# Rank scatter on one core: 14 of 128 tiles as row copies and all loads in halves of 10 KB

## The chip, the core and the metric

The kernel runs on one core of one Trainium2 chip. The metric is device time in microseconds (us) of one execution. "The span" is the time from the first to the last instruction in the profile, about 2 us less. Executions of the kernel before agree within 0.2%.

## The reference

```python
B, N, D = 8, 2048, 2560                      # x: B x N x D float32, scores: B x N
order = np.argsort(scores, axis=1)
ranks = np.argsort(order, axis=1)            # rank of each row within its batch
out[np.arange(B)[:, None], ranks, :] = x     # row i of a batch goes to row rank(i)
```

16,384 rows of 10 KB are read and written once, each to a place that the scores decide. Ranks are counted on VectorE by comparing every score of a batch with all others; that part is done by about 435 us and is not on the path at the end. What matters here is how rows are moved.

## The kernel before

There are two ways for a row. The *bulk* works in groups of 256 rows (2 tiles of 128): GpSimd issues a load into SBUF, 20 KB a partition, and two indirect DMAs that scatter the rows by rank. The *row copies* go from DRAM to DRAM, one DMA a row, issued by SyncE and ScalarE, with the target's address in a register.

```python
GROUPS = [(256 * i, 2) for i in range(8)]        # (first row, rows a partition)
DIRECT = range(6)                                # batches whose group 0 is row copies
BULK = [(b, g) for b in range(B) for g in range(len(GROUPS)) if g or b not in DIRECT]
NBUF, LAG, G = 8, 4, 16
THIN = [(b, 4) for b in range(1, B)]             # groups whose scatter skips 4 partitions
HOLES = range(48, 48 + 4)                        # those partitions: 8 single row copies a group
HALVED = range(8)                                # bulk groups loaded in two DMAs of 10 KB a partition
# ... load of bulk group k:
for j in range(m if k in HALVED else 1):
    part = slice(j * D, (j + 1) * D) if k in HALVED else slice(0, m * D)
    line.eng.dma_start(out=xb[k % NBUF][:, part], in_=rows[:, part]).then_inc(sem, 16)
# ... row copies; the two sequencers, sp (SyncE) and act (ScalarE), take half a group each:
todo = list(enumerate(THIN))
for b in DIRECT:
    while todo and todo[0][1][0] < b:
        n, where = todo.pop(0)
        thin_rows(n, *where)                     # single row copies, sp and act in turns
    for h, (line, name) in enumerate(((sp, ENG.SP), (act, ENG.Activation))):
        line.after(dve, t_rows[b])
        half = WIDE // 2                         # 128
        with line.eng.Fori(0, half // G) as q:   # a loop on the sequencer
            _, at = nc.values_load_multi_w_load_instructions(   # 16 addresses to registers
                rows_i[b][:, bass.ds(half * h + q * G, G)], engines=[name], ...)
            for i in range(G):
                row = b * N + GROUPS[0][0] + half * h + i
                line.eng.dma_start(
                    out=out_bytes[bass.ds(at[i], ROW)],
                    in_=x_bytes[bass.ds(q * (G * ROW) + row * ROW, ROW)],
                ).then_inc(s_rows[line], 16)
for n, where in todo:
    thin_rows(n, *where)
```

## Time and profile before

| | kernel before |
|---|---|
| time, median (range) | 782.2 us (782.1 to 783.2) |
| span of the profiled run | 779.7 us |
| row copies: SyncE, ScalarE | 800, 792 |
| bulk groups | 58 |
| last row copy issued / last bulk packet / last row packet | 765 / 769.4 / 775.4 us |

The prediction below shows the page's DMA rows, one stretch of the DMA view and the order of time of the two issuing queues. In the DMA view, q0 is the bulk, q1 and q10 are the row copies of SyncE and ScalarE; its columns are packets, MB, and the time of those packets as a share of 16 engines. In the order of time a line is: start, length, engine, source line, operation, tensors, count. "SPq" and "ACTq" are the sequencers of SyncE and ScalarE. L402 is the DMA of the looped row copies, L376 that of the single ones, L391 the load of 16 addresses into registers.

### The profile page before, as it was taken

The numbers are of one execution on the slowest core, as the hardware profiler recorded it, in microseconds if no ns is written. First come the engines' busy times: TensorE is split into PE (matmuls) and PEld (weight loads), VectorE is DVE, ScalarE is ACT, GpSimd is POOL, SyncE is SP. The second block draws the span as 40 slices with busy tenths as digits, with TensorE's granted clock in tenths as the row PEclk, the third lists the DMA queues.
The fourth block names the chain that finished last, engine by engine and source line by source line (L and its number), as shares of the span: only waits on it lengthen the run. The fifth ranks groups of instructions, "written<-read, shape, count | busy, mean of one in ns | idle before, by whom it ended". The sixth has DMA issues, their size and how long they took to land.

```text
span 779.7 us, 8177 instructions
## 1 busy us (share of the span) xinstructions
PE 35.4 (5%) x170; PEld 30.5 (4%) x170; DVE 399.8 (51%) x825; ACT 0.0 (0%) x1; POOL 150.2 (19%) x189
## 2 busy tenths in 40 slices
PE   4000020020020020120000000000000000000000
PEld 4000010010010010120000000000000000000000
DVE  5999979979979979899999200000000000000000
ACT  0000000000000000000000000000000000000000
POOL 4113122212121211112121212121212121220100
PEclk9999995555555555565555555555555555555555
DMA  8999999999999999999999999999999999999995
GB/s 360 418 419 419 426 415 425 415 421 416 424 418 424 416 421 417 425 417 423 419 421 420 422 419 421 420 422 422 417 425 416 426 416 425 417 424 418 419 415 101
DMA packets 77186, 320.15 MB, mean 411 GB/s; under 512 B 28448, under 2 KB 53920, under 8 KB 53920
## 3 DMA queue, kind: packets, MB, share of 16 engines
q0 software_dynamic: 25920, 300.90, 90.7%
q1 hardware_dynamic: 25904, 10.93, 5.5%
q10 hardware_dynamic: 25344, 8.16, 4.5%
q14 instruction: 17, 0.14, 0.0%
q8 instruction: 1, 0.02, 0.0%
HBM read 168.41 MB, written 168.35 MB: 432 GB/s over the span
## 4 chain that ended last, share of the span: by engine, by line
DMA 49%; another core or an unknown queue 19%; DVE 13%; POOL 7%; issue 6%; PE 1%; POOLq 0%; SPq 0%
DMA out_dram<-x,rank_i 43%; DVE trash L238 12%; DMA x<-in_x_dram 6%; POOL out_dram L422 5%; POOL x L126 1%; PE ps_all L196 0%; DVE s_all L339 0%; DMA s_in<-in_scores_dram 0%; PE ps_col L175 0%; POOLq L446 0%; DVE rank_i L276 0%; DVE rank L270 0%; DVE rank L264 0%; PE ps_row L298 0%
## 5 line engine op out<-in xcount | busy, mean ns | idle before, releaser
L238 DVE TENSOR_SCALAR_CACHE_REDUCE trash<-s_all,s_col 128x1792 bf16<-128x1792 f32 (+7 forms) x240 | 315.2, 1348 | 4.6
L422 POOL DMA_INDIRECT out_dram<-x,rank_i x116 | 112.7, 972 | 141.8 <-DMA x<-in_x_dram 36.4
L126 POOL DMA_DIRECT2D x<-in_x_dram x64 | 35.7, 560 | 445.7 <-DMA out_dram<-x,rank_i 426.6
L238 DVE SCALAR_TENSOR_TENSOR trash<-s_all,s_col,mask 128x256 bf16<-128x256 f32 x128 | 61.6, 481 | 0.0
L196 PE MATMUL ps_all<-ident,s_col 128*128 128x128 f32 x128 | 28.5, 416 | 3.1 <-DVE s_all L339 2.8
L196 PEld LDWEIGHTS ps_all<-ident,s_col 128*128 128x128 f32 x128 | 26.8, 226 | 4.2 <-DVE s_all L339 3.2
L298 PE MATMUL ps_row<-ident,rank 128*1 128x128 f32 x26 | 7.0, 366 | 392.5 <-DVE rank_i L284 335.2
L339 DVE COPY s_all<-ps_all 128x512 f32<-128x512 f32 x32 | 20.2, 685 | 1.7 <-PE ps_all L196 1.4
L238 DVE DVE_READ_ACCUMULATOR trash<-s_all,s_col 128x1 f32 x240 | 19.9, 83 | 0.0
L298 PEld LDWEIGHTS ps_row<-ident,rank 128*1 128x1 f32 x26 | 1.9, 95 | 395.8 <-DVE rank_i L284 337.6
L238 DVE DVE_READ_ACCUMULATOR trash<-s_all,s_col,mask 128x1 f32 x128 | 10.6, 83 | 0.0
L309 DVE TENSOR_SCALAR thin_i<-ps_row 1x8 int32<-1x8 f32 x7 | 1.1, 154 | 17.7 <-PE ps_row L298 17.7
L324 DVE TENSOR_SCALAR rows_i<-ps_row 1x256 int32<-1x256 f32 x6 | 2.5, 412 | 4.1 <-PE ps_row L298 4.1
L183 DVE COPY s_col<-ps_col 128x128 f32<-128x128 f32 x1 | 0.3, 290 | 4.5 <-PE ps_col L175 4.5
L175 PE MATMUL ps_col<-ident,s_in 8*128 8x8 f32 x16 | 2.1, 262 | 3.6 <-DMA s_in<-in_scores_dram 3.6
L175 PEld LDWEIGHTS ps_col<-ident,s_in 8*128 8x128 f32 x16 | 2.0, 211 | 3.6 <-DMA s_in<-in_scores_dram 3.6
L276 DVE CAST rank_i<-rank 128x16 int32<-128x16 f32 (+3 forms) x11 | 1.9, 173 | 0.4
L270 DVE TENSOR_TENSOR rank<-rank,acc 128x16 f32<-128x16 f32 (+3 forms) x11 | 1.9, 170 | 0.4
L264 DVE TENSOR_TENSOR rank<-acc,acc 128x16 f32<-128x16 f32 (+3 forms) x11 | 1.9, 170 | 0.4
L284 DVE TENSOR_SCALAR rank_i<-rank,hole 128x2 int32<-128x2 f32 x7 | 1.6, 228 | 0.2
L156 POOL TENSOR_SCALAR_AFFINE_SELECT mask<-mask 128x256 f32<-128x256 f32 x2 | 0.8, 398 | 0.0
L168 DVE MEMSET acc<- 128x128 f32 x1 | 0.2, 165 | 1.1 <-SPq L102 1.1
(10 smaller groups left out, 1.8 us busy)
## 6 DMA issues: line engine op xcount, KB each, us to landing
x<-in_x_dram POOLq DMA_DIRECT2D x50, 2560.0 KB
x<-in_x_dram POOLq DMA_DIRECT2D x14, 1280.0 KB
out_dram<-in_x_dram SPq DMA_DIRECT2D x800, 10.0 KB
out_dram<-in_x_dram ACTq DMA_DIRECT2D x792, 10.0 KB
x<-in_x_dram SPq DMA_DIRECT2D x2, 1280.0 KB, 9.3
out_dram<-x,rank_i POOLq DMA_INDIRECT x116, 48.4
s_in<-in_scores_dram SPq DMA_DIRECT2D x1, 64.0 KB
```

Of the source, the lines that this page charges most:

```text
L126: line.eng.dma_start(out=xb[k % NBUF][:, part], in_=rows[:, part]).then_inc(sem, 16)
L175: nc.tensor.transpose(out=ps_col[:, B * c:B * (c + 1)], in_=s_in[:, r + j:r + m * P:m], identity=ident[:B, :B],)
L196: nc.tensor.transpose(out=ps_all[:, P * c:P * (c + 1)], in_=s_col[:, c, b:b + 1].to_broadcast([P, P]), identity=ident[:],)
L238: do(out=trash[i][:, :P * (hi_c - lo_c)], in0=s_all[:, P * lo_c:P * hi_c], accum_out=acc[i][:, col:col + 1], **how,)
L264: nc.vector.tensor_tensor(out=rank[:, cols], in0=acc[0][:, cols], in1=acc[1][:, cols], op=OP.add)
L270: nc.vector.tensor_tensor(out=rank[:, cols], in0=rank[:, cols], in1=acc[2][:, cols], op=OP.add)
L276: nc.vector.tensor_copy(out=rank_i[:, cols], in_=rank[:, cols])
L284: nc.vector.tensor_scalar(out=rank_i[:, cols], in0=rank[:, cols], scalar1=hole[:], scalar2=None, op0=OP.add,)
L298: nc.tensor.transpose(out=ps_row[:1, P * j:P * (j + 1)], in_=rank[:, col:col + 1], identity=ident[:],)
L324: nc.vector.tensor_scalar(out=rows_i[b][:].rearrange("o (p j) -> o p j", p=P), in0=ps_row[:1, :WIDE].rearrange("o (j p) -> o p j", p=P), s ...
L339: nc.vector.tensor_copy(out=s_all[:, 512 * q:512 * (q + 1)], in_=ps_all[:, 512 * q:512 * (q + 1)],)
L422: nc.gpsimd.indirect_dma_start(out=out_flat, out_offset=bass.IndirectOffsetOnAxis(ap=rank_i[:, col:col + 1], axis=0), in_=xb[k % NBUF][:, ...
```

## The change

One more group of 256 rows and 8 more single rows go to the row copies, and all loads are cut in two. The intent is to take rows off the bulk's way through SBUF, and to give the row copies more turns on the DMA engines by making the bulk's packets smaller.

```diff
-    DIRECT = range(6)
+    DIRECT = range(7)
-    THIN = [(b, 4) for b in range(1, B)]
+    THIN = [(b, 4) for b in range(1, B)] + [(3, 6)]
-    HALVED = range(8)
+    HALVED = range(len(BULK))
-            while todo and todo[0][1][0] < b:
+            while todo and (todo[0][1][0] < b or b == DIRECT[-1]):
```

The last line moves the single row copies that are left ahead of the last loop.

## The prediction

> **What bounds the kernel now.** I read the page first, its DMA rows above all, then the DMA view cut to stretches, then the order of time of the two queues that issue the row copies, then single packets and single issues in the trace.
>
> ```profile
> DMA  8999999999999999999999999999999999999995
> GB/s 360 418 419 419 426 415 425 415 421 416 424 418 424 416 421 417 425 417 423 419 421 420 422 419 421 420 422 422 417 425 416 426 416 425 417 424 418 419 415 101
> ...
> q0 software_dynamic: 25920, 300.90, 90.7%
> q1 hardware_dynamic: 25904, 10.93, 5.5%
> q10 hardware_dynamic: 25344, 8.16, 4.5%
> ```
>
> The 16 DMA engines are full from the first slice to the last but one. q0 carries the bulk, issued by GpSimd: load a group of 256 rows into SBUF, scatter it by rank. q1 (SyncE) and q10 (ScalarE) carry the row copies, DRAM to DRAM, 800 and 792 of them. Those two are the short queues in bytes but not in packets, and the DMA view of 440 to 640 us shows why:
>
> ```profile
> DMA packets 19793, 84.05 MB, mean 420 GB/s; under 512 B 7349, under 2 KB 13945, under 8 KB 13945
> ...
> q0 software_dynamic: 6596, 79.77, 93.6%
> q1 hardware_dynamic: 6597, 2.12, 4.2%
> q10 hardware_dynamic: 6597, 2.12, 4.2%
> ```
>
> The three queues get the same number of packets: each engine serves them in turn, one packet each. A row is 16 pieces of 640 B, one an engine, and a semaphore write of 4 B behind each: two packets an engine. A group is 8 load packets of 20 KB, 16 scatter packets of 10 KB and 3 semaphore packets an engine, 27 in all, so a queue gets 13.5 rows through in each group's 13.2 us: 0.98 us a row. That is the service limit of a row queue.
>
> The other limit is issue, and the order of time of the two queues shows it:
>
> ```profile
> 19.44 233.36 SPq L402 DMA_DIRECT2D out_dram<-in_x_dram  x256
> ...
> 507.67 244.95 SPq L402 DMA_DIRECT2D out_dram<-in_x_dram  x256
> 753.57 11.37 SPq L376 DMA_DIRECT2D out_dram<-in_x_dram  x16
> 19.40 342.35 ACTq L402 DMA_DIRECT2D out_dram<-in_x_dram  x384
> ```
>
> A sequencer's first loops run at 233.36/256 = 0.91 and 342.35/384 = 0.89 us a row, its later ones at 0.96. Rows issued less rows served, counted by me from issues and 640 B packets, is 2 to 6 up to 120 us, grows from there, and stays at 32 to 34 in each queue from about 360 us. So up to 360 us a queue runs at the pace at which its sequencer can issue; only then is its ring full and the turn-taking sets the pace. One block of ScalarE, read off in order, shows the issue cost: 16 DMA instructions of 0.53 us, each with one ALU operation and two moves (0.09 us) and 0.12 us between them, 0.74 us a row; then 1.9 us for the branch and the load of 16 row addresses into registers. That is 13.7 us for 16 rows, 0.86 us a row, with nothing to wait for. The source view agrees:
>
> ```profile
> L402 ACTq DMA_DIRECT2D out_dram<-in_x_dram x768: 418/530/1403, 19.4 to 749.6; - x192
> L391 ACTq TENSOR_LOAD <-rows_i x48: 1007/1488/2682, 18.0 to 735.8; - x48
> ```
>
> The ends nearly coincide: SyncE issues its last row at 765 us, q0's last packet is at 769.4, q1's at 775.4, the span ends at 779.7. The kernel is balanced: bulk and row copies run out together.
>
> **What the Trainium skill says.** Page "DMA: Bandwidth & Descriptors". Section "Queues, rings and completion order": an engine goes round the queue rows it has work for, packet by packet; the trace agrees (6596, 6597, 6597), and here a packet is one piece of 640 B to 20 KB. Section "Issuing engines are not separate DMA queues": issuing from several engines saves only sequencer time, "which is usually small relative to the DMA itself". For these row copies the trace says the opposite: 0.86 us to issue a row whose 32 packets take 16 x (32 + 9) = 656 ns of engine time, 0.04 us on 16 engines. Section "Latency and other measured facts": a register load [...]has a floor of about 0.6 us; here it is 1.0 us for 16 addresses and up to 2.7.
>
> **The change part by part.**
>
> *More row copies.* Batch 6's first group moves from bulk to row copies: 128 rows more for each queue. One more group leaves out four partitions (8 rows, to ScalarE). Rows a queue: 7 x 128 + 32 = 928 on both, against 800 and 792. On the engines this is nearly free. Removed from q0: 256 row loads and 264 row scatters; added: 264 rows. A 10 KB scatter packet takes 385 ns, a 20 KB load 761, so a bulk row costs about 766 ns of engine time against 656 to 709 for a row copy (709 is the mean with its slow packets at the end). About -12 engine-us, under 1 us of time.
>
> *All loads halved.* 49 or 50 more groups load in packets of 10 KB. Two of 385 ns replace one of 761, 9 to 11 ns more (means 386.5 and 762.1); times 6400 packets is 58 to 70 engine-us, plus one semaphore packet an engine and group, 7. Over 16 engines +4 to +5 us. What it buys is turns: a group now has 16 + 16 + 4 = 36 packets an engine, so the service limit of a row queue goes from 0.98 to 0.775 us a row (a group would take 36 turns, 13.95 us, for 18 rows). This is plainly the intent: without it 928 rows could not be served in 780 us.
>
> *The bulk's end.* 28,864 packets of 386.5 ns and 3,680 of 9 ns on q0 and 110 us of q1's first loads make 11,300 engine-us, 706 us on 16 engines. Overlapping packets sum to 1.022 of the time in the middle; two row queues at 0.9 us a row take 0.098 of it; 706/0.924 = 764, plus the start at 6.7: the bulk ends at about 770 us, where it does now.
>
> *The rows' end.* The service limit falls below the issue cost, so the row queues become issue-bound for the whole run, and nothing in the change makes issuing cheaper. From 160 to 360 us, steady and with rings not yet full, the DMA view counts:
>
> ```profile
> out_dram<-in_x_dram SPq DMA_DIRECT2D x231, 10.0 KB
> out_dram<-in_x_dram ACTq DMA_DIRECT2D x227, 10.0 KB
> ```
>
> 200/229 = 0.87 us a row. Before 160 us it is slower, where GpSimd issues groups at twice the usual pace (7 us apart; blocks of 15 to 17 us against 13.5 to 14): 146 rows of SyncE by 160 us. The rest is 928 - 146 = 782 rows, times 0.87 = 680: last issue at 840. Corrections, estimated: the blocks' register loads (1.0 to 2.6 us) and DMA instructions lengthen with GpSimd's issues, which become four a group and not three, +0.01 us a row or +7; after 770 GpSimd and the bulk are gone and blocks should take 13.5, -3. Last issue at about 844. The last row then needs about 4 us to its packets (the first rows did: issued 19.4, first packet 23.3 to 23.7), and the kernel 4.4 us from its last packet to the end, as now (775.4 to 779.7): span about 852. Runs last 2 us longer than the span (781.5 for 779.7): about **854 us**, and 9% slower.
>
> *Single rows ahead of the last loop.* All eight address sets are ready by about 435 us, when VectorE ends; the queues get there at about 710, so nobody waits. It moves 32 rows a queue from the end to before the last loop and saves nothing while the issue stream is the path. VectorE gains two small operations (0.23 and 0.15 us), TensorE two transposes, off the path.
>
> **The rivals.**
> 1. *The bulk is the bound* and the rows fit beside it. Then only halving and tail count: +4 - 1, less up to 4 us of today's tail (770 to 775.4, where a few engines work off row copies at a DMA share of 0.27, 0.13, 0.06): 779 to 786 us. For it: engines 100% busy now, and service at 0.775 would finish 928 rows by 745. Against: rows would have to be issued at 0.82 us each from 19.4 to 780, and blocks with empty rings took 13.5 to 17 us for 16; none was under 13.1.
> 2. *Issue at its floor.* The slow blocks could be due to the ring after all, and vanish once service is faster. With 13.3 us a block: 56 x 13.3 = 745, four sets of single rows at 6.8 = 27, start 18: 790, plus 8 and 2: 800 us. For it: the fastest blocks, 13.2 to 13.5. Against: slow blocks at 60 to 130 us with a backlog of 2 to 8 rows, so no full ring.
> 3. *Issue gets worse.* The double pace of GpSimd's issues before 130 us made blocks of about 15.5. If four issues a group act like that throughout, 56 x 15.3 + 27 + 18 = 902 to the last issue before the bulk-free end takes some 8 off: 905 us. Against: four issues in 13.5 us are still well below six in 14.
>
> **Range and chances.** The centre is the measured steady issue rate; 0.84 us a row (the fastest steady stretch of 40 us has 48 rows, 0.83) gives 782 x 0.84 + 160 + 10 = 827, 0.90 gives 874. Range 826 to 880. Faster by 2% needs under 766.5, below even the bulk's end: 0.02. Within 2%, up to 798, needs every block at its floor: 0.06. Slower: 0.92.
>
> **What would show it.** Right: the page's DMA digits fall to 1 or 2 in the last four slices with GB/s in the tens; q0's last packet stands at 765 to 775 us; GpSimd's last scatter issue at 730 to 745; SyncE's and ScalarE's loops show 0.85 to 0.92 us a row and end after 820; q1 and q10 have fewer packets than q0 in a middle stretch, not equal ones; the rows issued and not served stay under 10. Wrong: equal packets on all three queues in the middle, or loops under 0.82 us a row (then rival 1 or 2), or q0's last packet well past 785 (the bulk itself got slower).

## The result

| | before | after |
|---|---|---|
| time, median (range) | 782.2 us (782.1 to 783.2) | 838.8 us (831.1 to 847.8) |
| ratio of fast runs, 95% interval | | 1.069 (1.060 to 1.078) |
| span of the profiled run | 779.7 us | 840.6 us |
| rows issued by SyncE, ScalarE | 800, 792 | 928, 928 |
| last bulk packet | 769.4 us | 763.4 us |
| last row packet | 775.4 us | 839.0 us |

The change costs 7%. Ratios here are the mean time of one kernel's fast runs over that of the other's fast runs of the same rounds, so not quite the ratio of the medians quoted. One run of four, at 847.8 us, counts as slow for being over 1.5% above the fastest; its granted clock, 0.522, is that of fast ones, so it may be no more than the far end of this spread.

The page after, its DMA rows (tenths of busy time in 40 slices of 21 us, GB/s, then the queues):

```profile
DMA  8999999999999999999999999999999999992111
GB/s 363 418 417 421 417 418 419 417 418 417 418 418 417 418 418 417 418 418 418 418 417 417 418 418 418 418 418 418 419 417 418 419 418 418 417 417 56 26 24 17
...
q0 software_dynamic: 32544, 295.58, 83.1%
q1 hardware_dynamic: 30000, 12.25, 5.6%
q10 hardware_dynamic: 29696, 9.56, 4.8%
```

For 36 slices the engines are as full as before; in the last three they move 17 to 26 GB/s. The view of stretches puts numbers on it (stretch, length, busy time by engine, clock, DMA share, GB/s):

```profile
740.00:750.00 10.00, 0.00 (x0) 0.00 (x0) 0.00 (x0) 0.00 (x0) 0.00 (x0) 0.50 1.03 417
765.00:780.00 15.00, 0.00 (x0) 0.00 (x0) 0.00 (x0) 0.00 (x0) 0.00 (x0) 0.50 0.17 25
800.00:820.00 20.00, 0.00 (x0) 0.00 (x0) 0.00 (x0) 0.00 (x0) 0.00 (x0) 0.50 0.15 24
```

From 765 us the engines are at least 83% idle and no compute engine works. What still works is the issuing, as the order of time of the two queues shows:

```profile
19.56 232.86 SPq L402 DMA_DIRECT2D out_dram<-in_x_dram  x256
...
492.41 223.75 SPq L402 DMA_DIRECT2D out_dram<-in_x_dram  x256
...
732.19 105.77 SPq L402 DMA_DIRECT2D out_dram<-in_x_dram  x128
...
719.77 106.60 ACTq L402 DMA_DIRECT2D out_dram<-in_x_dram  x128
```

The first loops run as before (232.9 us for 256 rows, before 233.4), the third at 0.87 us a row where the kernel before had 0.96, and the last one at 0.83, most of it with nearly empty DMA engines. SyncE issues its last row at 838.0 us and the span ends at 840.6. That the turns no longer bind shows in the DMA view of 440 to 640 us:

```profile
q0 software_dynamic: 8690, 78.88, 93.2%
q10 hardware_dynamic: 7470, 2.41, 4.8%
q1 hardware_dynamic: 7247, 2.33, 4.7%
```

Before, the three counts were equal. Now the row queues leave 14% and 17% of the turns unused. Rows issued less rows served, counted as in the prediction, stay under 7 throughout; before, from 360 us on, they were 28 to 35, in the median 32 or 33.

### The profile page after: what moved, and what is told of

It reads as the page before. It is cut to its first block, busy times and chain, and to the rows that moved or that the text cites. A ratio compares the mean times of both kernels' runs of the same rounds, so it can differ in the third digit from the quotient of the medians.

```text
span 840.6 us, 9343 instructions
## 1 busy us (share of the span) xinstructions
PE 36.3 (4%) x174; PEld 31.2 (4%) x174; DVE 400.7 (48%) x828; ACT 0.0 (0%) x1; POOL 177.6 (21%) x235
## 4 chain that ended last, share of the span: by engine, by line
DMA 58%; DVE 12%; another core or an unknown queue 7%; POOL 5%; issue 4%; PE 1%; POOLq 0%; SPq 0%
DMA out_dram<-x,rank_i 52%; DVE trash L238 11%; DMA x<-in_x_dram 5%; POOL out_dram L422 3%; POOL x L126 2%; PE ps_all L196 0%; DVE s_all L339 0%; DMA s_in<-in_scores_dram 0%; PE ps_col L175 0%; POOLq L446 0%; DVE rank_i L276 0%; DVE rank L270 0%; DVE rank L264 0%; PE ps_row L298 0%
## 5 line engine op out<-in xcount | busy, mean ns | idle before, releaser
L126 POOL DMA_DIRECT2D x<-in_x_dram x112 | 63.1, 566 | 416.2 <-DMA out_dram<-x,rank_i 414.0
```

## The experiments

All runs are beside runs of the kernel before on the same chip (medians 781.7 to 782.4 us there). The theory: the path is the sequencers' issue of the row copies. The rivals: the bulk or the DMA engines' turns set the time, or halving the loads is what costs. "Issue" stands here for all that a sequencer spends on a row while no full ring holds it, stretched DMA instructions included.

### Row copies alone

```diff
-BULK = [... if g or b not in DIRECT]
+BULK = [... if g or b not in DIRECT][:8]        # on the changed kernel; wrong result on purpose
```

> The changed kernel with the bulk cut to its first 8 groups of 57 (a wrong result on purpose): all 928 row copies a queue stay, with the bus nearly empty after some 60 us. Issue theory: the queues run at their floor, 56 blocks of 13.25 us and 4 sets of single rows of 6.5 us from 18 us on, last issue at about 786, time about 792 us, which is more than the whole kernel before. Rival (the DMA engines or their turn-taking set the pace of the rows): with the engines free the rows take far less, under 700 us.

Measured: 814.6 us (2 runs, 812.1 and 817.0), 4% above the whole kernel before. Its page and the order of time of SyncE:

```profile
DMA  8999941111111111111111111111111111111111
GB/s 363 417 418 422 393 150 25 24 26 24 26 24 26 24 25 24 24 25 24 26 24 26 25 25 24 24 24 24 24 26 24 26 24 26 27 26 24 25 25 24
```

```profile
19.46 232.06 SPq L402 DMA_DIRECT2D out_dram<-in_x_dram  x256
...
480.61 213.92 SPq L402 DMA_DIRECT2D out_dram<-in_x_dram  x256
...
707.87 104.46 SPq L402 DMA_DIRECT2D out_dram<-in_x_dram  x128
```

This settles the cause: with four fifths of the bytes taken away (61 MB are left of 318), 928 row copies a queue still take longer than everything did before. The expectation was 22 us low. Two parts of it were: the blocks of 16 rows took 20 to 21 us between 60 and 102 us, where GpSimd issues eight scatters in a row and for some 30 us after, and some loops have blocks of 13.6 us and not 13.25.

It also points to what slows the issue beside the bulk. The loads of 16 addresses (count, then shortest/median/longest in ns), here from 140 us on, when GpSimd is silent:

```profile
L391 ACTq TENSOR_LOAD <-rows_i x48: 1005/1021/1030, 144.7 to 799.6; - x48
L391 SPq TENSOR_LOAD <-rows_i x48: 970/976/992, 145.3 to 799.5; - x48
```

and in the changed kernel, first while the bulk runs:

```profile
L391 ACTq TENSOR_LOAD <-rows_i x52: 1006/1048/2545, 18.1 to 760.6; - x52
L391 SPq TENSOR_LOAD <-rows_i x51: 972/1193/2702, 18.1 to 758.8; - x51
```

Sorted by their start within a group of GpSimd's issues (on average 13.1 us long, issues in its first 4 us; 126 to 720 us), the 4 loads that start in the first 3 us take 2.5 to 2.6 us, the 15 that start 7 or 8 us in take 0.97 to 1.07, and the 8 that start after 11 us take 1.0 to 2.7.

This suggests that issue times depend on how the blocks of 13.2 to 15 us fall against GpSimd's groups. GpSimd's issue instructions are not all of it: in the run of row copies alone GpSimd issues nothing from 71 to 111 us, and yet the loads at 81 us took 2.1 us and the DMA instructions from 72 to 97 us about 1.0 us instead of 0.53, with only 2 to 5 rows waiting. What holds them there is open.

The blocks drift slowly past the groups, which would fit the changed kernel's spread of 2% from run to run, where the kernel before, held by turns for half its time, has 0.2%. That the drift is the spread's cause was not tested, and the run with the single rows last, below, is held by issue too and spreads by 0.2% only.

### The bulk alone, with halved and with whole loads

On the changed kernel all row copies are left out (wrong result); in the second run `HALVED = range(8)` as well.

> The changed kernel without any row copy (wrong result on purpose), all loads in halves of 10 KB: 11,290 us of engine time over 16 engines are 706 us, less about 1.5% for overlapping packets, plus 10 at both ends: about 708 us. Issue theory: 130 us below the changed kernel. Rival (the bulk sets the end of the changed kernel): 820 us or more.

> As e6_bulk_alone_10k, with the loads after the first 8 groups whole again, 20 KB a packet. By packet times (385 ns against half of 761, 128 x 49 packets, and one semaphore packet less) 4.7 us below e6_bulk_alone_10k: about 703 us. If the halves cost nothing, the same as e6.

Measured: 715.7 us (715.4 to 716.0) with halves, 714.2 us (713.8 to 714.6) with whole loads. The bulk is 120 us short of the changed kernel's time and cannot be its bound. Both are above what was expected, by 8 and 11 us, in part because packets overlap less than thought: from 100 to 700 us their times sum to 1.009 and 1.005 of the engines' time, where 1.015 was expected. Halving costs 1.4 us, not the 4.7 expected: packet times on q0 differ by 55 us, 3.4 us on each of 16 engines, a part of which the larger overlap takes back, and the last packet comes 2 us later. Without row copies the whole loads' packets took 768 ns on average and not the 762 they took beside them.

### More rows without the halves

```diff
-HALVED = range(len(BULK))
+HALVED = range(8)                                # on the changed kernel
```

> The changed kernel with the loads after the first 8 groups whole again (20 KB): service falls to 0.98 us a row, so up to the bulk's end at about 761 us some 794 rows of a queue are issued instead of 834, and the other 134 follow at 13.25 us for 16: about 877 us, 35 to 40 us over the changed kernel. If the rows are held by the issue alone and turns play no part: as the changed kernel, 831 to 848 us.

Measured: 873.4 us (873.4 to 873.5). So halving is worth 37 us (of the fast runs) once there are seven batches of row copies. With whole loads the turns are scarce again, and the third and the last loop show both limits one after the other, 0.96 us a row beside the bulk and 0.82 after it:

```profile
504.15 245.96 SPq L402 DMA_DIRECT2D out_dram<-in_x_dram  x256
...
764.34 104.46 SPq L402 DMA_DIRECT2D out_dram<-in_x_dram  x128
```

### The halves without more rows

```diff
-HALVED = range(8)
+HALVED = range(len(BULK))                        # on the kernel before
```

> The kernel before with all loads in halves, nothing else changed (800 and 792 rows). Issue theory: the rows are issue-bound from start to end and done at about 730 us as the changed kernel had issued 800 rows of SyncE by 730; then the bulk alone sets the end, with 4 to 5 us more packet time and without the tail of row copies: 777 to 782 us, the same as before within 1%. Rival (halving itself is what costs the time): 800 us or more.

Measured: 777.6 us (777.1 to 777.7), ratio 0.994 (0.993 to 0.996). Halving is not what costs the time; alone it gains 0.6%. But the expected way there was wrong: SyncE's last row was issued at 770.5 us, not 730.

```profile
19.65 244.40 SPq L402 DMA_DIRECT2D out_dram<-in_x_dram  x256
...
273.98 244.27 SPq L402 DMA_DIRECT2D out_dram<-in_x_dram  x256
```

That is 0.95 us a row, with 1 to 7 rows waiting, so it is issue in the sense above and not turns. Its DMA instructions and register loads were longer than in the changed kernel (from 140 to 700 us: 0.60 against 0.55 us, and 1.88 against 1.33 us, on ScalarE). Up to 250 us both kernels have the same loads, scatters and row copies in the same order, and yet the first loop takes 244.4 us here and 232.9 there. Why is open; neither turns nor the number of rows explains it.

### A cheaper issue

```diff
-                with line.eng.Fori(0, half // G) as q:
+                for q in range(half // G):       # unrolled in the program; on the changed kernel
```

> The changed kernel with the loops of 16 rows unrolled in the program, so that source addresses are constants: the single rows, which have that form already, took 0.64 us a row where a row in the loop takes 0.74, and there is no branch. Issue theory: a block of 16 takes about 11.2 us with an idle GpSimd and 12 beside it, the rows keep up with their service limit of 0.775 us and end by about 745, before the bulk: 774 to 780 us, 7% below the changed kernel and a little below the kernel before. Rival (issue is not what holds the changed kernel): 831 us or more.

Measured: 776.4 us (776.3 to 776.6), correct; ratio to the kernel before 0.993 (0.991 to 0.994). This is the changed kernel with the same bytes, packets and rows, 60 us faster, and of the kernels with a correct result it is the fastest; that it is 1 us ahead of the halves without more rows says that the extra row copies gain next to nothing. The page's DMA rows and the order of time:

```profile
DMA  8999999999999999999999999999999999999994
GB/s 359 420 416 417 417 415 419 417 415 417 418 416 417 416 417 415 417 416 417 417 416 416 418 417 417 416 416 416 416 417 417 417 416 417 417 417 417 416 421 209
```

```profile
438.45 196.54 SPq L402 DMA_DIRECT2D out_dram<-in_x_dram  x256
...
648.43 94.80 SPq L402 DMA_DIRECT2D out_dram<-in_x_dram  x128
```

The loops take 0.74 to 0.81 us a row; rows end at about 750 us and the last bulk packet, at 770.9, sets the end. From 440 to 640 us the row queues leave only 2% and 4% of the turns unused (8570, 8380, 8249 packets), so turns are nearly used up here. The source address is now a constant: one move and no ALU operation a row, and no branch. The views of line L402, first of the changed kernel and then of this one, for 896 rows (count, then shortest/median/longest in ns):

```profile
L402 SPq MOVE out_dram<-in_x_dram x1792: 29/29/103, 19.4 to 837.4; - x200
L402 SPq ALU_OP  x848: 32/33/55, 19.3 to 837.3; - x170
```

```profile
L402 SPq MOVE out_dram<-in_x_dram x896: 3/29/710, 19.0 to 742.6; - x180
```

A row without a stall takes 0.63 to 0.64 us where the loop takes 0.74 and more.

### The cheaper issue without the halves

`HALVED = range(8)` on the unrolled kernel.

> The changed kernel with its loops unrolled, as e3_unrolled, but with the loads after the first 8 groups whole again (20 KB). Issue is now cheap (0.70 us a row with an idle GpSimd), turns are scarce (0.98 us a row). If both limits are real and the slower one counts: some 808 rows of a queue issued at the bulk's end near 761 us, the other 120 at 0.70 us each, about 850 us (840 to 860), 75 us above e3_unrolled. If e3_unrolled was fast for its cheap issue alone and halving adds nothing: 775 to 780 us.

Measured: 845.0 us (844.5 to 845.6). The DMA view of 440 to 640 us has equal counts again, and 29 to 36 rows, in the median 32 or 33, wait in each queue from 240 us on:

```profile
q0 software_dynamic: 6585, 79.76, 93.6%
q1 hardware_dynamic: 6585, 2.12, 4.2%
q10 hardware_dynamic: 6585, 2.12, 4.2%
```

With this the four combinations at seven batches are complete, and both limits are real (the 0.775 is the estimate of the prediction; no run stood at it):

| | loop (issue 0.83 us a row on idle engines, 0.84 to 0.91 beside the bulk) | unrolled (0.70 on idle engines, 0.74 to 0.81 beside the bulk) |
|---|---|---|
| whole loads (0.96 us a row by turns, measured) | 873.4 us | 845.0 us |
| halved loads (0.775 us a row by turns, estimated) | 838.8 us (fast runs 836.2) | 776.4 us |

### 32 rows a turn of the loop

```diff
-    G = 16
+    G = 32                                        # on the changed kernel
```

> The changed kernel with 32 rows a loop turn instead of 16. The register load takes 0.55 us for 8 addresses and 1.0 for 16, so it should take 1.9 for 32: only the branch (0.4 us) and a part of the slow loads go away, 28 times some 0.5 to 0.9 us. Issue theory: 14 to 25 us below the changed kernel, 812 to 824 us. If the DMA engines set the pace: no difference.

Measured: 828.0 us (815.5 to 828.9), two of four runs counted as slow; ratio of the fast ones 1.050 (1.041 to 1.059). The fast ones are 815.5 and 827.5 us, on average 15 us below the fast runs of the changed kernel: a gain, as expected of a cheaper issue, and at the lower end of the 14 to 25 us expected. The two that count as slow (828.5 and 828.9 us) do so by the rule of 1.5% alone, at the granted clock of the others, so the size of the gain stays unclear. The load of 32 addresses has a median of 2.8 us on ScalarE and up to 5.1 on SyncE, so little more than the branch was saved.

### The single row copies last, as before

```diff
-while todo and (todo[0][1][0] < b or b == DIRECT[-1]):
+while todo and todo[0][1][0] < b:                  # on the changed kernel
```

> The changed kernel with the single row copies in the order of the kernel before (those of batches 5 to 7 and the new set after the last loop). Issue theory: the same number of rows through the same two sequencers, so the same within the changed kernel's own spread of 831 to 848 us. Rival (the single rows ahead of the last loop wait for their addresses or hold the last loop up): faster by the length of that wait.

Measured: 843.4 us (842.1 to 843.8), no faster than the changed kernel (fast runs 831.1 to 842.4). The order of the single rows is not the cause of the loss; whether the new order gains a few us is lost in the spread.

### Some halves

```diff
-HALVED = range(8)
+HALVED = range(24)                                # on the kernel before
```

> The kernel before with 24 groups halved instead of 8. e1_halved_only (all halved) took 4.8 us off the kernel before, and the bulk alone costs 1.4 us more with all halves. If the gain is that the row copies no longer trail the bulk, it needs only some of the turns: 24 groups should do as well as all, 776 to 780 us. If it comes with each halved group: 781 us.

Measured: 778.9 us (778.1 to 779.5), ratio 0.996 (0.995 to 0.998). A third of the groups halved gives about two thirds of the gain of all halves. That fits what was expected: what halving gains in the kernel before is that the row copies stop trailing the bulk. Here the last row packet is at 771.6 us, 0.3 us after the last bulk packet; in the kernel before it came 6 us after.

## Why the prediction was right

It named 854 us, with a range of 826 to 880; measured were 838.8, and 842.4 in the profiled run. By its steps (the times are of the profiled run; its difference from the median is the spread):

- **Turns.** Right: equal counts go once the loads are halved, and come back when they are whole. The four combinations show the two limits apart.
- **Issue becomes the path.** Right: the rows waiting stay under 7, the loops run at 0.83 to 0.91 us a row, and a cheaper issue alone takes 60 us off.
- **The bulk's end.** Predicted 770 us, measured 763.4. The 11,300 us of packet time were right (11,293 in the trace). What was off is the share of the engines left to them, 0.924, which the trace has at 0.93 (packet times sum to 1.026 from 100 to 700 us, of which the row queues have 0.094); that is nearly the whole difference. It had no part in the time, as the bulk does not set the end.
- **The rows' end.** Last issue predicted 844 us, measured 838.0. By 160 us SyncE had issued 153 rows and not 146, which is 6 us; the other 775 took 678 us, 0.875 us a row, and the sum with its corrections had the same (684 us for 782 rows). That match is in part luck: from 160 to 360 us the two queues issued a row in 0.88 us on average, 0.01 more than before, as corrected, but from 440 to 640 us in 0.87, and that four GpSimd issues a group are the reason was not tested.
- **The end.** The sum allowed 8 us after the last issue; it took 2.6. A row's 4 us to its packets was read under a full load; on idle engines the last row took 1.0 (838.0 to 839.0 us). And the 4.4 us from the last packet to the end were 1.6.
- **Readings.** Two counts of waiting rows were too narrow: a recount every 0.25 us gives 1 to 10 up to 120 us where the prediction has 2 to 6, and 28 to 35 from 360 us on where it has 32 to 34. Neither enters the sum.
- **Rivals.** The bulk-bound case (779 to 786 us) needed a cheaper issue, and something like it came about only with one, at 776.4, just below that range. Issue at its floor (800) failed even with the bulk gone: 814.6. The third (905) did not come about.
- **Single rows ahead of the last loop.** Predicted to be neutral; it was, within the spread.

## What to carry to other kernels

In these kernels a queue of small DMAs has two rates: what its sequencer can issue and what the engines' turns serve. Count both before giving it more work, and look at how many issued DMAs wait: here 28 to 36 said turns, 1 to 7 said issue. A change that lifts one limit (smaller packets elsewhere) gains only up to the other, and here the other was mostly the work of a loop: a move and an ALU operation a row and a branch a turn, which unrolling removed.

## What the Trainium skill lacked or had wrong

- Page "DMA: Bandwidth & Descriptors", section "Issuing engines are not separate DMA queues": that issue time is "usually small relative to the DMA itself" does not hold for row copies. Issue took 0.83 us a row on idle engines, against about 0.04 us of all 16 engines for its packets, and set the time of the changed kernel.
- Same page, section "Queues, rings and completion order": the turns by packet are right (6585, 6585, 6585), and the packets of 9 to 17 descriptors that it calls typical did not show: the trace records a row copy as two packets an engine and a scatter as nine, and still all three queues had the same number in a stretch. The section gives no depth of a row's ring; issued rows stopped piling up at 36 at most, in the median 32 or 33, two packets each on an engine.
- Same page, section "Latency and other measured facts": the floor of about 0.6 us for a `tensor_load` is close for 8 addresses (0.53 to 0.55 us with GpSimd silent). That page does not say that the time grows with their number, 0.97 to 1.03 us for 16, nor that it stretches beside the bulk, to 2.7 us in the changed kernel.
- Same page, section "Rules for kernel authors" advises 1 MiB or more a DMA for bandwidth. Loads of 2.6 MB and halves of 1.3 MB both keep to it, so no run here tests it. What it lacks is that the size of a packet decides how many turns other queues get: the halves cost 1.4 us in 714 with the bulk alone and gained 37 us beside the row copies.
